# Last mixer of a two-block transformer on one core: the low parts of its weights formed by an accumulating DMA in SBUF

## The chip, the cores and the metric

The kernel runs on one NeuronCore of a Trainium2 chip. The metric is the device time of one launch in microseconds (us). The engines have these names in the profile: PE is TensorE, DVE is VectorE, ACT is ScalarE, POOL is GpSimd and SP is SyncE; PEld is the weight load of TensorE. A queue from which transfers are issued is called after its engine (SPq, POOLq).

## The reference, cut to what matters

Eight sublayers follow one another on 512 tokens of width 1024, all in fp32: MLA attention, feed-forward, differential attention, feed-forward, an even mixer, feed-forward, an odd mixer, feed-forward. The change concerns the odd mixer, the last of the four mixers:

```python
def odd_mixer(x, w_in, forget_b, dw_w, dw_b, cn_g, cn_b, w_out):
    p = x @ w_in
    q, k, v = ...                                     # 8 heads of 64 channels
    log_f = jax.nn.log_sigmoid(p[..., 3 * D_C:3 * D_C + H_C] + forget_b)
    y_c = forgetting_attention(q, k, v, log_f)        # logit += cum[t] - cum[s], causal
    y_d = conformer_conv(p[..., 3 * D_C + H_C:], dw_w, dw_b, cn_g, cn_b)
    return jnp.concatenate([y_c, y_d], axis=-1) @ w_out

def conformer_conv(p_d, dw_w, dw_b, cn_g, cn_b):
    h = p_d[..., :D_D] * jax.nn.sigmoid(p_d[..., D_D:])
    h = causal_dwconv(h, dw_w) + dw_b                 # 31 taps on each of 512 channels
    return jax.nn.silu(layer_norm(h, cn_g, cn_b))
```

## The kernel before, in words

Every fp32 product is made on TensorE from three products of a rounded high part and a remainder, the low part (lines 370 to 372: high times high, high times low, low times high). The weights come in units of 128 x 1024 (512 KB), or 128 x 528 (264 KB) for the first four units of the values. `Weights` keeps a plan of all units in the order of use. For each unit, `load` issues one transfer from DRAM into a raw tile on SP (line 162), and `split` makes the high part on ACT (line 169, a copy into the narrower type fp32r) and the low part (line 170, raw minus high) on DVE, for some units on POOL. The pool of raw tiles, `wraw`, has two buffers; `whi` and `wlo` have five each. So a raw tile is loaded when the one two units earlier has been read for the last time.

The odd mixer uses 26 such units after its first four. Those first four (`od_a` and `od_g` in the plan) and the next four named `od_x` are loaded from one tensor, `in_od_d`, for the convolution; then come `od_v` (values, four short units first and two long ones later), `od_q` and `od_k` (four head pairs each) and `od_o` (the output projection, eight). In the order of the plan: v 1 to 4 (short), x 1 to 4, q and k of pair 0, q and k of pair 1, v 5 and 6, q and k of pair 2, q and k of pair 3, o 1 to 8. In this text x 1 is the first `od_x` unit, q 0 the `od_q` unit of pair 0, and so on. All 26 low parts are made on DVE before.

Around them run these steps. `log_sigmoid` makes the log forget gates (an exponential on ACT, line 1480, then short DVE operations). `sums` adds them up with two matmuls (lines 1500 and 1501), ACT rounds the sums (`cumh`, line 1511), and `spread` writes them into the tiles `ab` on DVE (lines 1539 to 1542). `rows` transposes `ab` on PE (line 1549). `place` copies q and k of a head pair into stacked tiles: `qq` and `kb` by ACT (line 1418), the other half `kk` by a further ACT copy (line 1425). The scores of a head (lines 1588 to 1590) need all of these; ACT makes their softmax (lines 1603 and 1599) with short DVE operations between (lines 1602 and 1595), PE turns them over (line 1052) and multiplies them with the values.

The 124 taps of the convolution (lines 1368 and 1370, one DVE instruction each) lie between all this on DVE. A few run early; the rest stand behind `spread`. A scheduler that simulates the engines fixes the order of the instructions on each engine when the kernel is built; each engine then goes through its list strictly in that order, waiting on semaphores.

Of the kernel before, what the change touches and what calls it, by code (L numbers as in the profile page):

```python
# [9 lines left out]
F32 = mybir.dt.float32  # L10
F32R = mybir.dt.float32r
BF16 = mybir.dt.bfloat16
AF = mybir.ActivationFunctionType
OP = mybir.AluOpType
# [38 lines left out]

ONPOOL = ("uq_n", "ukv", "df_o", "mla_o")
OTHERWISE = (11, 12, 15, 20, 23, 24, 25, 73, 79, 80, 81, 82, 83, 84, 85, 86, 88, 90, 91, 100, 102, 103)
NORM_ACT = (1, 3, 6, 7, 12, 13, 16, 24, 25, 26, 30)
ROPE_POOL = (1, 2, 3, 4, 5, 7, 9, 11)
DUP_ACT = (0, 2, 4, 6)
# [83 lines left out]
class Weights:  # L142
# [23 lines left out]
    def split(self, pool, raw, o, n, eng):  # L166
        tiles = [p.tile([P, UNIT], F32R, name="w" + k, tag="w" + k) for p, k in zip(pool, ("hi", "lo"))]
        hi, lo = [x[:, :n] for x in tiles]
        self.nc.scalar.activation(hi, raw[:, o:o + n], AF.Copy)  # L169
        eng.tensor_sub(lo, raw[:, o:o + n], hi.bitcast(F32))  # L170
        return tiles

    def steps(self):

        while self.loaded < min(len(self.plan), self.at + 2) and (
                self.loaded == self.at or self.plan[self.loaded][0] != "win" or self.sums is not None):
            self.load()
        name, raw, n = self.got[self.at]
        self.at += 1
        nc = self.nc  # L180
        if name != "win":
            on_pool = (name in ONPOOL) != (self.at - 1 in OTHERWISE)
            self.ready.append((name, *self.split((self.hi, self.lo), raw[0], 0, n, nc.gpsimd if on_pool else nc.vector)))
            return

        gate, up = raw
        H = UNIT // 2
        a11, a12, a21, a22 = gate[:, :H], gate[:, H:], up[:, :H], up[:, H:]
        pg = self.split((self.hi, self.lo), gate, 0, UNIT, nc.vector)
        yield  # L190
        pu = self.split((self.hi, self.lo), up, H, H, nc.vector)
        nc.vector.tensor_add(a22, a21, a22)
        nc.vector.tensor_sub(a21, a11, a21)
        yield
        su = self.split(self.sums, up, 0, UNIT, nc.vector)
        nc.vector.tensor_sub(a11, a22, a11)
        nc.vector.tensor_sub(a12, a12, a11)
        yield
        sg = self.split(self.sums, gate, 0, UNIT, nc.vector)

        def part(tiles, o):
            return [x[:, o:o + H].rearrange("p (k n) -> p k n", n=P) for x in tiles]

        self.ready.append((name, {
            1: part(pg, 0), 2: part(pg, H), 3: part(sg, H), 4: part(pu, 0), 5: part(su, H), 6: part(sg, 0), 7: part(su, 0)}, None))
# [107 lines left out]
def kernel(ctx: ExitStack, tc: tile.TileContext, a: dict, out: bass.AP):  # L313
# [393 lines left out]
    def ffn(xpool_cm, xT, key, i, ps, names):  # L707
# [3 lines left out]
        with pool("ffn") as fp:  # L711
# [3 lines left out]
            def hidden(j, g, u):  # L715
                nc.vector.tensor_mul(g, g, u)
                h = fp.tile([P, S], F32R, name="hh", tag="hh", bufs=HID)
                l = fp.tile([P, S], F32R, name="hl", tag="hl", bufs=HID)
                split(h, l, g)
                chunks[j] = (h, l)  # L720
# [112 lines left out]
    def mla(xT, close_x, open_x, names):  # L833
        with pool("mla_o") as op_:
            cmask = op_.tile([P, S], F32, name="cmask")
            with ExitStack() as st:
# [28 lines left out]
                def turn_c(j, h, l):  # L865
                    ps = pst()
                    for t in range(NT):
                        nc.tensor.transpose(ps[:, t * P:(t + 1) * P], cq[:, t, j * P:(j + 1) * P], ident)
                    split(h, l, ps, par("g_q", j) if j < 3 else par("g_kv", j - 3))
# [67 lines left out]
                def head(h):  # L937
                    p, i = divmod(h, 2)
                    if i == 0:
                        WP[p] = W.next("uq_n", 3, 256), W.next("ukv", 2, 512)  # L940
                    wq, wk = WP[p]
                    m = slice(i * P, (i + 1) * P)
                    got = []
                    for s, (w, k, x, sc) in enumerate((
                            (wq, 3, (cqh, cql), -MLA_SCALE),
                            (wk, 2, (ckh, ckl), None))):
                        ps = acc()
                        project_T(ps, w, x, k, m=m)
                        hi = ap_.tile([P, S], F32R, name="qh", tag=f"qh{s}", bufs=2)
                        lo = ap_.tile([P, S], F32R, name="ql", tag=f"ql{s}", bufs=2)  # L950
                        split(hi, lo, ps, sc)
                        got += [hi, lo]
                    Q[h] = got
# [39 lines left out]
                def rest(h, pt, qb, n, e, sums):  # L993
                    nc.vector.reciprocal(sums[:, 2:3], sums[:, 1:2])
                    if 4 * h + qb in NORM_ACT:
                        nc.scalar.activation(e[:, :n], e[:, :n], AF.Copy, scale=sums[:, 2:3])
# [905 lines left out]
```

## Time and profile before

| | |
|---|---|
| median of 3 runs | 2256.09 us (2255.45 to 2257.32) |
| the profiled execution | 2255.44 us, of which the span from the first to the last instruction is 2253.7 us |
| mean granted clock of TensorE | 0.993 of full speed |
| PE busy | 2194.6 us, 97% of the span, 14076 matmuls |
| DVE busy | 1753.4 us, 78% |
| ACT busy | 998.2 us, 44% |
| POOL busy | 132.1 us, 6% |

The shares are means over the whole span. The profiled execution is 0.65 us below the median of the runs. The odd mixer occupies about 1660 to 1891 us of the span.

### The profile page before, as it was taken

To read this page: it belongs to the slowest core of one execution; us is meant where nothing else is said; L and a number is where in the kernel's file an instruction comes from. 1 tells how busy PE (TensorE), PEld (TensorE's weight loads), DVE (VectorE), ACT (ScalarE), POOL (GpSimd) and SP (SyncE) were. 2 spreads that over 40 slices of the span, in tenths; PEclk is the share of its full clock that TensorE was granted. 3 is DMA by queue.
4 is the path that set the end of the run, shared out by engine and by line. 5 is a ranking of instruction groups with operands and counts; after the bars stand their busy time and mean duration, and the time that the engine had idled before them with its cause. 6 is when DMAs were issued, how large, how long until landed. Compare 5 with 4: busy or idle time off the path is not lost. (4 is left out here: it accounts for less than half of the span.)

```text
span 2253.7 us, 35104 instructions
## 1 busy us (share of the span) xinstructions
PE 2194.6 (97%) x14076; PEld 1971.3 (87%) x14076; DVE 1753.4 (78%) x2871; ACT 998.2 (44%) x1669; POOL 132.1 (6%) x138
## 2 busy tenths in 40 slices
PE   8999999999999999999999999999999889999997
PEld 8888999998988789999988899999988767999996
DVE  5767988887666688888765588888679987988886
ACT  4654444333665554443333244433336655444331
POOL 2200000001321100000010000000010000000001
PEclk9999999999999999999999999999999899999999
DMA  5213332332321133333323233333232102233331
GB/s 174 64 48 103 94 113 94 113 94 75 111 79 63 47 108 107 104 94 113 94 98 95 75 131 107 104 100 108 90 99 93 57 19 103 94 113 94 113 94 56
DMA packets 59363, 210.48 MB, mean 93 GB/s; under 512 B 6624, under 2 KB 6880, under 8 KB 59200
## 3 DMA queue, kind: packets, MB, share of 16 engines
q1 hardware_dynamic: 56304, 198.97, 27.8%
q0 software_dynamic: 2320, 8.23, 1.1%
q8 instruction: 110, 1.80, 0.3%
q10 hardware_dynamic: 576, 1.05, 0.1%
q14 instruction: 53, 0.43, 0.1%
HBM read 206.12 MB, written 2.10 MB: 92 GB/s over the span
## 5 line engine op out<-in xcount | busy, mean ns | idle before, releaser
L169 ACT ACTIVATE whi<-wraw 128x1024 fp32r<-128x1024 f32 (+2 forms) x528 | 520.4, 988 | 838.8 <-PE acc L371 501.7
L170 DVE TENSOR_TENSOR wlo<-wraw,whi 128x1024 fp32r<-128x1024 f32 (+2 forms) x502 | 568.2, 1133 | 126.2 <-ACT whi L169 123.3
L371 PE MATMUL acc<-xl,whi 128*128 128x256 f32 (+1 forms) x1712 | 522.9, 305 | 3.5 <-DVE xl L480 3.5
L372 PE MATMUL acc<-xh,wlo 128*128 128x256 f32 (+1 forms) x1712 | 522.2, 305 | 2.6 <-DVE wlo L170 2.5
L370 PE MATMUL acc<-xh,whi 128*128 128x256 f32 (+1 forms) x1712 | 523.6, 306 | 0.4 <-DVE kl L1097 0.4
L371 PEld LDWEIGHTS acc<-xl,whi 128*128 128x128 f32 x1712 | 322.5, 188 | 29.2 <-DVE xl L480 4.7
L370 PEld LDWEIGHTS acc<-xh,whi 128*128 128x128 f32 x1712 | 322.4, 188 | 25.6 <-DVE kl L1097 0.5
L372 PE MATMUL acc<-xs,wlo 128*128 128x256 f32 x1216 | 341.3, 282 | 0.0
L371 PE MATMUL acc<-xql,whi 128*128 128x256 f32 x1216 | 341.0, 281 | 0.0
L372 PEld LDWEIGHTS acc<-xh,wlo 128*128 128x128 f32 x1712 | 322.6, 188 | 18.9 <-DVE wlo L170 3.8
L370 PE MATMUL acc<-xs,whi 128*128 128x256 f32 x1216 | 339.0, 280 | 0.0
L371 PEld LDWEIGHTS acc<-xql,whi 128*128 128x128 f32 x1216 | 228.5, 188 | 5.5
L370 PEld LDWEIGHTS acc<-xs,whi 128*128 128x128 f32 x1216 | 229.6, 189 | 3.5
L372 PEld LDWEIGHTS acc<-xs,wlo 128*128 128x128 f32 x1216 | 228.1, 188 | 0.3
L370 PE MATMUL tr<-whi,hh 128*128 128x512 f32 (+1 forms) x296 | 117.8, 398 | 0.0
L781 DVE TENSOR_TENSOR sums<-sums,acc 128x512 f32<-128x512 f32 x76 | 52.3, 688 | 83.9 <-PE acc L372 83.3
L371 PE MATMUL tr<-wlo,hh 128*128 128x512 f32 (+1 forms) x296 | 116.8, 395 | 0.0
L372 PE MATMUL tr<-whi,hl 128*128 128x512 f32 (+1 forms) x296 | 115.8, 391 | 0.0
L372 PE MATMUL ps<-whi,hl 128*128 128x512 f32 x288 | 113.7, 395 | 0.0
L370 PE MATMUL ps<-whi,hh 128*128 128x512 f32 x288 | 113.4, 394 | 0.0
L371 PE MATMUL ps<-wlo,hh 128*128 128x512 f32 x288 | 113.2, 393 | 0.0
L430 DVE SCALAR_TENSOR_TENSOR res<-res,acc 128x512 f32<-128x512 f32 x87 | 59.1, 683 | 58.1 <-PE acc L372 57.7
(364 smaller groups left out, 3959.5 us busy)
## 6 DMA issues: line engine op xcount, KB each, us to landing
wraw<-in_gu_dram SPq DMA_DIRECT2D x176, 512.0 KB, 3.5
wraw<-in_dn_dram SPq DMA_DIRECT2D x88, 512.0 KB, 3.4
wraw<-in_ev_in_dram SPq DMA_DIRECT2D x16, 512.0 KB, 3.5
wraw<-in_mla_o_dram SPq DMA_DIRECT2D x8, 512.0 KB, 3.5
wraw<-in_df_q_dram SPq DMA_DIRECT2D x8, 512.0 KB, 3.5
wraw<-in_df_k_dram SPq DMA_DIRECT2D x8, 512.0 KB, 3.5
wraw<-in_df_v_dram SPq DMA_DIRECT2D x8, 512.0 KB, 3.5
wraw<-in_df_o_dram SPq DMA_DIRECT2D x8, 512.0 KB, 3.4
```

The lines of the kernel that those rows point to most:

```text
L169: self.nc.scalar.activation(hi, raw[:, o:o + n], AF.Copy)
L170: eng.tensor_sub(lo, raw[:, o:o + n], hi.bitcast(F32))
L370: nc.tensor.matmul(ps, ah, bh, start=first, stop=False)
L371: nc.tensor.matmul(ps, ah, bl, start=False, stop=False)
L372: nc.tensor.matmul(ps, al, bh, start=False, stop=last)
L430: nc.vector.scalar_tensor_tensor(y, y, ALPHA if first else 1.0, ps, op0=OP.mult, op1=OP.add, accum_out=SUMS[t][:, c:c + 1] if sums else None)
L781: nc.vector.tensor_add(g[:, 1:3], g[:, 1:3], v)
```

## The change

For the five names of the odd mixer listed in `BYDMA`, the low part is no longer made by DVE. ACT writes minus the high part into the low tile (a copy with scale -1.0, from the raw tile), and a transfer issued on POOL's queue adds the raw tile to it, from SBUF to SBUF. Line numbers rise by 1 behind the new tuple and by 5 behind `split`.

```diff
+BYDMA = ("od_x", "od_v", "od_q", "od_k", "od_o")
...
         self.nc.scalar.activation(hi, raw[:, o:o + n], AF.Copy)
-        eng.tensor_sub(lo, raw[:, o:o + n], hi.bitcast(F32))
+        if eng is None:
+            self.nc.scalar.activation(lo, raw[:, o:o + n], AF.Copy, scale=-1.0)
+            self.nc.gpsimd.dma_start(lo.bitcast(F32), raw[:, o:o + n], accum_op=OP.add)
+        else:
+            eng.tensor_sub(lo, raw[:, o:o + n], hi.bitcast(F32))
...
-            self.ready.append((name, *self.split((self.hi, self.lo), raw[0], 0, n, nc.gpsimd if on_pool else nc.vector)))
+            self.ready.append((name, *self.split((self.hi, self.lo), raw[0], 0, n, None if name in BYDMA else nc.gpsimd if on_pool else nc.vector)))
```

The scheduler's order changes with it. On SP, these are the loads of v 3, v 4, x 1, x 2 and x 3 before (`DVE` in the waits is the low part of the unit two earlier, `DMAHW` an earlier load):

```order
L162 DMA wraw_16881<-in_od_v0_dram 128x528 [waits DMAHW7_49,DVE_49]
L162 DMA wraw_16887<-in_od_v0_dram 128x528 [waits DMAHW0_49,DVE_49]
L162 DMA wraw_17166<-in_od_d_dram 128x1024 [waits DMAHW1_49,DVE_49]
L162 DMA wraw_17196<-in_od_d_dram 128x1024 [waits DMAHW2_49,DVE_49]
L162 DMA wraw_17266<-in_od_d_dram 128x1024 [waits DMAHW3_49,DVE_49]
```

and the same loads in the changed kernel:

```order
L163 DMA wraw_16882<-in_od_v0_dram 128x528 [waits DMAHW7_49,DMASW1_49,Activation_49]
L163 DMA wraw_16889<-in_od_v0_dram 128x528 [waits DMAHW0_49,DMASW2_49,Activation_49]
L163 DMA wraw_17169<-in_od_d_dram 128x1024 [waits DMAHW1_49,DMASW3_49,Activation_49]
L163 DMA wraw_17200<-in_od_d_dram 128x1024 [waits DMAHW2_49,DMASW4_49,Activation_49]
L163 DMA wraw_17271<-in_od_d_dram 128x1024 [waits DMAHW3_49,DMASW5_49,Activation_49]
```

Their number and order stay; the semaphore of DVE is replaced by that of ACT and of the accumulating transfer (`DMASW`) that reads the raw tile.

On ACT, this is where the k parts of head pair 0 are placed, before (`whi_17700` is the high part of q 2, read from its raw tile `wraw_17640`):

```order
L169 ACTIVATE whi_17700<-wraw_17640 128x1024 [waits DMAHW5_49,PE_49]
L1418 ACTIVATE kb00_17069<-acc_17574 64x512 [waits PE_49]
L1418 ACTIVATE kb01_17073<-acc_17574 64x512
L1425 ACTIVATE kk00_17070<-kb00_17069 64x512 [waits Activation_49]
L1425 ACTIVATE kk01_17074<-kb01_17073 64x512 [waits Activation_49]
```

and in the changed kernel, where `whi_17655` and `wlo_17656` belong to v 6 and `whi_17714` and `wlo_17715` to q 2:

```order
L172 ACTIVATE wlo_17656<-wraw_17630 128x1024 [waits DMASW1_49]
L1423 ACTIVATE kb00_17072<-acc_17585 64x512 [waits PE_49]
L1423 ACTIVATE kb01_17076<-acc_17585 64x512
L170 ACTIVATE whi_17714<-wraw_17653 128x1024 [waits DMAHW5_49]
L172 ACTIVATE wlo_17715<-wraw_17653 128x1024 [waits DMASW2_49]
L1430 ACTIVATE kk00_17073<-kb00_17072 64x512 [waits Activation_49]
```

The high part of q 2 has moved from ahead of the `kb` copies to between them and the `kk` copies, and its negation stands there too.

On PE, this is where `rows` transposes `ab`, before (`whi_17433` is the high part of q 0):

```order
L370 MATMUL acc_17537<-xh_16571,whi_17433 128x512
L371 MATMUL acc_17537<-xl_16572,whi_17433 128x512
L1549 MATMUL tr_17442<-ident_76,ab1_17109 128x128 [waits DVE_49,Pool_49]
L1549 MATMUL tr_17437<-ident_76,ab0_17108 128x128 [waits DVE_49]
L1549 MATMUL tr_17437<-ident_76,ab0_17108 128x128 x3
```

and in the changed kernel (`whi_17322` is the high part of x 4):

```order
L375 MATMUL acc_17482<-xh_16571,whi_17322 128x512
L376 MATMUL acc_17482<-xl_16572,whi_17322 128x512
L1554 MATMUL tr_17451<-ident_76,ab1_17112 128x128 [waits DVE_49,Pool_49]
L1554 MATMUL tr_17446<-ident_76,ab0_17111 128x128 [waits DVE_49]
L1554 MATMUL tr_17446<-ident_76,ab0_17111 128x128 x3
```

The transposes have moved forward by more than a unit: from within the matmuls of q 0 to behind the first 8 of the 24 matmuls of x 4. In the same way the matmuls of `sums` have moved from x 3 to ahead of the last matmul of x 2, and on ACT `cumh` now stands behind the negation of k 0, the exponential of the gates behind that of x 3. On POOL the accumulating transfers of all units but the last stand, in the order of the plan, right behind the copy of `mkb` (line 1341 before, 1346 now).

## Rows read from the trace of the kernel before

**Rows 1.** The page: busy time of each engine.

```profile
PE 2194.6 (97%) x14076; PEld 1971.3 (87%) x14076; DVE 1753.4 (78%) x2871; ACT 998.2 (44%) x1669; POOL 132.1 (6%) x138
```

**Rows 2.** Stretches of the odd mixer: busy time of each engine, granted clock, DMA share.

```profile
core 0: us, PE busy (x) PEld busy (x) DVE busy (x) ACT busy (x) POOL busy (x), PEclk, DMA share, GB/s
...
1700.00:1778.50 78.50, 78.05 (x419) 65.02 (x417) 77.05 (x137) 51.09 (x98) 0.00 (x0) 1.00 0.26 81
1778.50:1781.90 3.40, 0.06 (x1) 0.00 (x0) 3.40 (x7) 3.35 (x7) 0.00 (x0) 0.94 0.00 0
1781.90:1795.10 13.20, 11.82 (x42) 9.63 (x42) 12.72 (x28) 8.93 (x22) 0.00 (x0) 0.50 0.15 41
1795.10:1844.20 49.10, 39.36 (x210) 29.20 (x208) 44.22 (x107) 32.02 (x92) 0.00 (x0) 0.96 0.00 1
1844.20:1870.00 25.80, 23.18 (x102) 18.62 (x103) 16.16 (x25) 9.21 (x12) 1.05 (x1) 0.93 0.26 82
```

**Rows 3.** Waits of PE, 1778 to 1845: total us, times, longest.

```profile
PE tr L1052 <- ACT e L1599: 5.1, 7, 1.3
PE ps L1588 <- ACT e L1603: 4.1, 5, 3.4
```

**Rows 4.** Waits of ACT in the same stretch.

```profile
ACT e L1599 <- DVE sums L1595: 8.6, 8, 1.9
```

**Rows 5.** Groups of DVE by line and shape, 1709 to 1845.

```profile
L1370 DVE SCALAR_TENSOR_TENSOR cv<-gl,sm,cv 128x512 f32<-128x512 f32 x98 | 69.4, 741 | 0.4
L170 DVE TENSOR_TENSOR wlo<-wraw,whi 128x1024 fp32r<-128x1024 f32 x12 | 14.6, 1215 | 0.0
```

**Rows 6.** Timeline of SP: start, duration, what is issued.

```profile
1672.41 11.17 SPq L162 DMA_DIRECT2D wraw<-in_od_d_dram  x4
1685.71 10.82 SPq L162 DMA_DIRECT2D wraw<-in_od_qk_dram  x4
```

**Rows 7.** Timeline of DVE; the idle time before in brackets.

```profile
1671.67 0.71 DVE L170 TENSOR_TENSOR wlo<-wraw,whi 128x528 fp32r<-128x528 f32 x1 [2.13 <-ACT whi L169]
...
1684.46 1.22 DVE L170 TENSOR_TENSOR wlo<-wraw,whi 128x1024 fp32r<-128x1024 f32 x1
...
1708.94 0.27 DVE L1542 TENSOR_TENSOR ab<-cumh,lf 128x64 f32<-128x64 f32 x1
```

**Rows 8.** Timeline of ACT.

```profile
1668.15 0.65 ACT L169 ACTIVATE whi<-wraw 128x528 fp32r<-128x528 f32 x1 [5.44 <-PE acc L371]
...
1679.99 1.06 ACT L169 ACTIVATE whi<-wraw 128x1024 fp32r<-128x1024 f32 x1 [1.63 <-DMA wraw<-in_od_d_dram]
...
1708.27 0.23 ACT L1511 ACTIVATE cumh<-lf 128x32 fp32r<-128x32 f32 x1 [1.23 <-DVE lf L1510]
...
1726.39 1.27 ACT L1425 ACTIVATE kk<-kb 64x512 fp32r<-64x512 f32 x2
```

**Rows 9.** Timeline of POOL.

```profile
1663.62 0.82 POOL L1341 CAST mkb<-cst 128x128 bf16<-128x128 f32 x1 [2.59 <-DMA cst<-in_cst_dram]
```

**Rows 10.** Transfers: count, KB each, median us from issue to landing; and SP's loads as a share.

```profile
q1 hardware_dynamic: 56304, 198.97, 27.8%
...
wraw<-in_od_d_dram SPq DMA_DIRECT2D x8, 512.0 KB, 3.5
...
lng<-in_ln_ffn_g_dram POOLq DMA_DIRECT2D x4, 512.0 KB, 4.8
...
wraw<-in_od_v_dram SPq DMA_DIRECT2D x4, 264.0 KB, 2.7
```

**Rows 11.** Timeline of PE: matmuls 7, 8 and 9 of x 4; the first use of `kk`.

```profile
1706.88 0.40 PE L370 MATMUL acc<-xh,whi 128*128 128x512 f32 x1
1707.12 0.40 PE L371 MATMUL acc<-xl,whi 128*128 128x512 f32 x1
1707.35 0.40 PE L372 MATMUL acc<-xh,wlo 128*128 128x512 f32 x1
...
1729.15 0.22 PE L1589 MATMUL ps<-kk,qq 128*128 128x128 f32 x1
```

**Rows 12.** Timeline of PE: the first score behind its longest wait.

```profile
1781.94 0.47 PE L1588 MATMUL ps<-kb,qa 128*128 128x128 f32 x1 [3.38 <-ACT e L1603]
```

## The prediction, made before the changed kernel ran

> **What bounds the kernel now.** I began with the busy times of the page: PE is busy 97% of the span and DVE 78% [rows 1]. These are means over eight sublayers, so the next view cuts the odd mixer into stretches [rows 2]. From 1700 to 1778.5 us two engines are full at once: PE works 78.05 of 78.5 us and DVE 77.05. PE sets the pace there; DVE is full because the convolution's taps, which nobody needs yet, fill every gap. Up to 1778.5 DVE is therefore no bound, and whatever is taken from it there buys no time at that place.
>
> Behind it PE loses time. In the three stretches from 1778.5 to 1844.2 it stands still for 3.3 + 1.4 + 9.7 = 14.5 us, and the granted clock costs more: 13.2 us at 0.50, the lower of its two levels (1.2 against 2.4 GHz), lose 6.6 us and 49.1 us at 0.96 lose 2.0. Together that is 23.1 us [rows 2]. The half-clock stretch follows a single wait of PE of 3.38 us [rows 12]. PE's waits there are named: for the normed exponentials of ACT 5.1 us, for ACT's exponential itself 4.1 us [rows 3]. ACT in turn waits 8.6 us, in 8 waits, for the reciprocal on DVE [rows 4], a tiny operation that stands in DVE's list between taps: 98 taps (69.4 us) and 12 low parts (14.6 us) run on DVE from 1709 to 1845 [rows 5]. Here, and only here, a relieved DVE can shorten the kernel.
>
> The third view is the timelines around the loads. The low part of v 3 ends at 1671.67 + 0.71 = 1672.38, that of x 3 at 1685.68 [rows 7], and SP issues the next load into the same raw tile 0.03 us later in both cases (1672.41 and 1685.71) [rows 6]. So SP waits for nothing but the last reader of a raw tile, and of those there are two. One turn of a raw tile now takes a load (3.5 us [rows 10]), a high part (1.06 [rows 8]) and a low part (1.22 [rows 5]), 5.8 us; two tiles give a unit every 2.9 us at best, and PE takes one every 24 x 0.23 = 5.6 us (matmuls follow 0.23 us apart [rows 11]). The prologue has twice what it needs.
>
> **The change part by part.** DVE loses 26 low parts, 22 of 1.22 us and 4 of 0.71. Up to 1778.5 this is worth nothing, as said. ACT gains 26 negations; I cost one like the high part, the same copy of the same tile: 1.06 us, 0.65 for a short unit [rows 8]. ACT is busy 51.09 of 78.5 us [rows 2], so that its time as such hides; its order is what counts (below). POOL only issues; it is busy 6% [rows 1] and its transfers stand in the order of the units.
>
> The real edit is to the turn of a raw tile. It is now: load 3.5, high 1.06, negation 1.06, and then the landing of the accumulating transfer, which I call L (L' for a short unit): L + 5.62. No row shows such a transfer. The bounds: not below the 3.5 us that SP's 512 KB take; not above twice the 4.8 us of a plain 512 KB on POOL's queue, 9.6 [rows 10]. Between them I start from 4.8, the same queue, size and issuing engine, and add a second reading of the bytes, since the operation must read the low tile as well as the raw tile. SP's 198.97 MB took 27.8% of the 16 engines' span of 2253.7 us, so 0.524 MB cost 0.278 x 2253.7 x 0.524 / 198.97 = 1.65 us [rows 10]. L = 6.45; with half of that addition L' = 5.65. A unit then comes every (6.45 + 5.62) / 2 = 6.0 us, against the 5.6 that PE takes: the prologue no longer overtakes PE.
>
> The Trainium skill states in "Collectives: The Full Stack", "Why ReduceScatter is half of AllGather", that an adding transfer is slower because it reads two sources (measured 62.28 against 32.35 GB/s). No row here shows an adding transfer; an estimate that puts this whole ratio on 4.8 us gives 9.3 us, and the sum would be about 2291.
>
> A slower prologue costs time where something on PE's path stands behind it. Low parts do not: by the second chain below that of q 1 is there at 1690.9 + 2L' + 4L = 1728, where PE is due at some 1722.5 (65 matmuls of 0.23 us behind the one at 1707.35 [rows 11]) and late itself by then. But ACT works in order, and two of its copies now stand behind negations:
>
> First, `cumh` stands behind the negation of k 0. That unit's raw tile goes v 2, v 4, x 2, x 4, k 0. The high part of v 2 is made at 1668.15, held by PE [rows 8], so its negation ends at 1669.45; four turns later, 2L' + 2L + 4.0 + 3 x 5.62 (a short load of 2.7 [rows 10], 0.65 and 0.65 in the first), k 0 is negated at 1690.3 + 2L' + 2L. Then `cumh`, 0.23, and `spread`, from 1708.27 to 1709.21 in all 0.94 [rows 7, 8]: 1691.5 + 2L' + 2L = 1715.7. PE wants the transposes of `ab` behind the eighth matmul of x 4, at 1707.4 [rows 11]: a wait of 8.3 us. (The matmuls of `sums`, earlier in PE's list, wait for the gates, behind the negation of x 3; that wait is a part of the 8.3 and not additional.)
>
> Second, `kk` of pair 0 stands behind the negation of q 2. Its raw tile goes v 1, v 3, x 1, x 3, q 0, q 1, v 5, q 2. POOL's first transfer can't be issued before the copy of `mkb` ends at 1664.44 [rows 9]. Seven turns: 1664.44 + 4.0 + 6 x 5.62 + 2L' + 5L = 1702.2 + 2L' + 5L, then 0.64 for the copy (half of two in 1.27 [rows 8]): 1746.35. PE needs it at 1729.15 [rows 11]: 17.2 us in all, of which 8.3 are waited for already. Behind q 2 the heads use a unit more slowly than 6 us, so that the loop falls behind no further.
>
> PE so takes two waits of over 8 us. Long waits lowered the clock here: the one of 3.38 us was followed by 6.6 us of loss, and the stretch from 1844.2, at 0.93 of 25.8 us, lost 1.8 [rows 2, 12]. I take the middle, 4.2, twice: 8.4 us.
>
> On the other side, from 1709 to 1845 DVE is rid of 14.6 us [rows 5], so the taps end earlier and the reciprocals come sooner. Of the 23.1 us lost there the whole can come back at most; part of the waits are ACT's own exponentials, which nothing shortens [rows 3]. I take half, 11.6 us.
>
> Sum against the profiled execution: 2255.4 + 17.2 + 8.4 - 11.6 = 2269.4. That execution is 0.65 us below the median, so the median is predicted at 2270.
>
> **The rivals.** *A quick transfer (the other side).* If adding costs nothing beyond the plain 4.8, the two waits shrink to 3.3 and 7.25 us in all. They cost the clock little (1.8 each), and since PE is barely late, DVE's relief arrives nearly whole in the heads, say 20 us: 2255.4 + 7.25 + 3.6 - 20 = 2246. For it: SP's transfers, at 3.5, are even faster, and 16 engines are used by a quarter there [rows 2, 10]. The point from which it decides: with 11.6 returned and 3.6 lost by the clock, the wait must stay below 8.0 us, which is L of about 5.1. The Trainium skill ("DMA: Bandwidth & Descriptors", "Anatomy of one DMA — SWDGE (gpsimd) path") fits 2.0 us + bytes / 436e3, an estimate of 3.2 us for 512 KB; by it this rival holds, but the trace's 4.8 on this queue is above it.
>
> *A slow transfer.* L = L' = 9.6: 1702.8 + 2 x 9.6 + 5 x 9.6 = 1770.0, a wait of 40.9 us; 2255.4 + 40.9 + 8.4 - 11.6 = 2293. For it: no row shows what adding costs in the transfer engines; against it: they stand idle for three quarters of that time.
>
> *The tail gives back everything.* The waits are as I say, but the heads lose nothing any more, since DVE had been the last of their causes: 2255.4 + 17.2 + 8.4 - 23.1 = 2258, no change. For it: ACT's 8.6 us behind DVE [rows 4] and the single 3.38 us wait whose clock loss is the largest piece. Against it: ACT gives PE its waits by name [rows 3], and it gets more work.
>
> **How the numbers follow.** My forecast has a chance of 0.46, the quick transfer 0.20, the slow one 0.17, the full return 0.17. Within 0.2% (4.5 us, about what a measurement of this kernel can tell from no change) falls most of the full return, and some of the quick one and of mine: 0.17. Faster: most of the quick transfer and a little of the full return, 0.22. Slower 0.61. The range goes from 2247 to 2292, which leaves out about half of the quick case and half of the slow one. The forecast's own range, by half or double the clock loss and a quarter to three quarters of the return, is 2260 to 2280.
>
> **What would show it.** The landing of the accumulating transfers decides: 6.45 us supports the sum, 5 or less the quick rival, 9 or more the slow one. SP should issue each load right behind such a landing, and ACT's high parts should wait for loads where they waited for PE. PE should show a wait of some 8 us at the matmuls of `sums` and the transposes of `ab` together, another of 9 at `kk` of pair 0, and half clock behind them. In the heads PE's idle time should be near 7 us instead of 14.5, with fewer waits of ACT for reciprocals. I am wrong if PE keeps its 99% up to the first scores, or if low parts, and not copies on ACT, are what it waits for.

## The result and the profile after

The changed kernel takes 2273.02 us (median of 4 runs, 2272.26 to 2273.76) against 2256.04 us before: a ratio of 1.0074, 95% interval [1.0057, 1.0092]. It is slower by 17 us, as forecast (2270). The profiled execution took 2272.56 us with a span of 2270.8 us.

The page's first line, as [rows 1]: DVE has lost 26 us of work, ACT gained 21 and POOL 22, and PE does the same work in a longer time.

```profile
PE 2196.6 (97%) x14076; PEld 1973.0 (87%) x14076; DVE 1727.2 (76%) x2845; ACT 1019.6 (45%) x1695; POOL 154.0 (7%) x164
```

The stretches of the odd mixer, with the columns of [rows 2], are cut anew, since PE's work comes later. By PE's timeline, v 5 is first used at 1765 us here and was at 1736 before; the stretches up to 1765 hold what is ahead of it:

```profile
1660.00:1700.00 40.00, 37.98 (x281) 35.80 (x280) 17.62 (x33) 17.63 (x26) 8.83 (x19) 1.00 0.62 148
1700.00:1718.40 18.40, 11.38 (x49) 8.37 (x47) 10.16 (x36) 8.02 (x9) 2.13 (x3) 0.99 0.73 164
1718.40:1740.00 21.60, 21.57 (x91) 17.78 (x92) 16.84 (x27) 12.49 (x17) 2.34 (x3) 0.93 0.75 171
1740.00:1765.00 25.00, 13.74 (x50) 9.87 (x50) 18.49 (x32) 17.47 (x28) 3.44 (x4) 0.74 0.63 147
1765.00:1800.00 35.00, 35.00 (x219) 30.64 (x219) 30.49 (x61) 28.96 (x60) 4.30 (x5) 0.99 0.56 138
1800.00:1861.50 61.50, 53.29 (x281) 42.12 (x280) 51.48 (x127) 48.71 (x127) 2.58 (x3) 0.92 0.24 58
```

In the four stretches up to 1765 PE is idle for 2.0 + 7.0 + 0.0 + 11.3 = 20.3 us, and the granted clock (0.99, 0.93 and 0.74 in the last three) costs another 0.2 + 1.5 + 6.5 = 8.2. Before, nearly nothing was lost there (0.4 us idle from 1660 to 1736, at full clock). In the heads (1800 to 1861.5) 8.2 us are idle and 4.9 lost by the clock, 13.1 together, against the 23.1 of before: 10 us have come back.

PE's waits from 1660 to 1765 (total, times, longest):

```profile
PE tr L1554 <- DVE ab L1545: 5.6, 1, 5.6
PE ps L1594 <- ACT kk L1430: 4.8, 1, 4.8
PE ps L1593 <- ACT kb L1423: 4.0, 1, 4.0
PE ps L1593 <- ACT e L1608: 2.5, 1, 2.5
PE acc L377 <- DMA wlo<-wraw: 2.3, 2, 1.6
PE ps L1505 <- PE acc L376: 0.8, 1, 0.8
```

The first wait is for `ab`, behind `cumh`; the next two are for the placing of k of pair 0, and the 2.5 us behind them for the first exponentials of the heads. The low parts themselves cost 2.3 us. The cause stands one view further, in the timelines of SP, POOL and ACT:

```profile
1704.31 20.83 SPq L163 DMA_DIRECT2D wraw<-in_od_qk_dram  x4
...
1704.14 0.86 POOL L173 DMA_DIRECT2D wlo<-wraw  x1 [5.71 <-ACT wlo L172]
1711.14 0.86 POOL L173 DMA_DIRECT2D wlo<-wraw  x1 [6.13 <-ACT wlo L172]
1717.99 1.04 POOL L173 DMA_DIRECT2D wlo<-wraw  x1 [5.99 <-ACT cumh L1516]
...
1715.69 1.06 ACT L170 ACTIVATE whi<-wraw 128x1024 fp32r<-128x1024 f32 x1 [4.85 <-DMA wraw<-in_od_qk_dram]
1716.65 1.04 ACT L172 ACTIVATE wlo<-wraw 128x1024 fp32r<-128x1024 f32 x1
1717.60 0.21 ACT L1516 ACTIVATE cumh<-lf 128x32 fp32r<-128x32 f32 x1
...
1748.72 1.06 ACT L170 ACTIVATE whi<-wraw 128x1024 fp32r<-128x1024 f32 x1 [3.29 <-DMA wraw<-in_od_qk_dram]
1749.68 1.04 ACT L172 ACTIVATE wlo<-wraw 128x1024 fp32r<-128x1024 f32 x1
1750.74 1.28 ACT L1430 ACTIVATE kk<-kb 64x512 fp32r<-64x512 f32 x2
```

The four loads of q and k take 20.83 us where they took 10.82 [rows 6]. ACT waits for the load of k 0, makes its high part and negation, and only then `cumh`; the same with q 2 and `kk`. Before, the high part of k 0 waited for PE and not for a load:

```profile
1693.86 1.06 ACT L169 ACTIVATE whi<-wraw 128x1024 fp32r<-128x1024 f32 x1 [1.20 <-PE acc L371]
```

POOL's rows show a second thing: each accumulating transfer is issued at the same moment as a load, since the landing that frees one raw tile and the negation of the other fall together. SP's four loads, merged in its row, are issued at 1704.31, 1711.24, 1718.14 and 1724.81, each within 0.2 us of a transfer. The view of the low tiles gives the landings of the transfers issued from 1700 to 1730, and of those from 1855 to 1877, where few loads run:

```profile
DMA to landing us min/median/max: 6.8/7.0/8.3
...
DMA to landing us min/median/max: 4.4/4.5/6.3
```

### The profile page after: what moved, and what is told of

Read it like the earlier page. It is cut to its first block, busy times and chain, and to the rows that moved or that the text cites. A ratio compares the mean times of both kernels' runs of the same rounds, so it can differ in the third digit from the quotient of the medians.

```text
span 2270.8 us, 35167 instructions
## 1 busy us (share of the span) xinstructions
PE 2196.6 (97%) x14076; PEld 1973.0 (87%) x14076; DVE 1727.2 (76%) x2845; ACT 1019.6 (45%) x1695; POOL 154.0 (7%) x164
## 3 DMA queue, kind: packets, MB, share of 16 engines
q0 software_dynamic: 6064, 20.84, 4.0%
## 5 line engine op out<-in xcount | busy, mean ns | idle before, releaser
L175 DVE TENSOR_TENSOR wlo<-wraw,whi 128x1024 fp32r<-128x1024 f32 (+2 forms) x476 | 538.6, 1132 | 115.0 <-ACT whi L170 114.2
L393 POOL TENSOR_TENSOR lnr<-lnv,mhalf 128x1 f32<-128x1 f32 x32 | 24.4, 761 | 1274.2 <-DVE lnv L391 1274.1
```

The costliest lines, as they stand in the source:

```text
L393: nc.gpsimd.tensor_tensor(r[:, :n], v[:, :n], mhalf[:, :n], op=OP.pow)
```

## The experiments

The theory: with an accumulating transfer a raw tile is held until the transfer has landed; there are two; so the loads come every 6.8 us, and two copies on ACT that PE needs stand behind negations that wait for loads ("tile held"). The rivals: the 26 negations on ACT and the scheduler's new order do it ("negations"), or the adding as such is so slow that the transfer engines are the limit ("price of adding"). The expectations use this last name in two senses: the transfer is long because it adds, or the engines' own time is what the kernel waits for. Only the second contradicts the theory.

**Without the transfers.** In `split`, low parts stay minus the high part:

```diff
             self.nc.scalar.activation(lo, raw[:, o:o + n], AF.Copy, scale=-1.0)
-            self.nc.gpsimd.dma_start(lo.bitcast(F32), raw[:, o:o + n], accum_op=OP.add)
```

> The changed kernel without the accumulating transfers: the low parts of these 26 units stay minus the high part, so the low products are left wrong and only the time is read. Theory 'tile held': the raw tile is free after the negation, a turn is 5.6 us for two tiles, PE's waits at the sums, the transposes and kk vanish (under 2 us together) and DVE's relief stays: about 2246 us (2236 to 2251). Rival 'negations': the waits stay, 2265 or more.

Measured: 2246.84 us, 0.9958 of before [0.9943, 0.9973]. PE's waits from 1660 to 1765 are these two:

```profile
PE acc L376 <- DVE wlo L174: 0.4, 1, 0.4
PE ps L1592 <- ACT e L1607: 0.3, 1, 0.3
```

All 26 negations are there. The scheduler's order differs from the changed kernel's, but `cumh` and `kk` stand behind negations here too (of q 1 and q 2). So the negations make none of the waits, the relief of DVE, less whatever the negations cost, is worth 9 us, and the transfers cost 26.

**A plain copy in place of the adding one.**

```diff
-            self.nc.gpsimd.dma_start(lo.bitcast(F32), raw[:, o:o + n], accum_op=OP.add)
+            self.nc.gpsimd.dma_start(lo.bitcast(F32), raw[:, o:o + n])
```

> The changed kernel with a plain copy from SBUF to SBUF in place of the adding one, on the same queue and of the same size: the low parts become copies of the raw tile, so only the time is read. Theory 'tile held, queueing behind the load': packets fall from 328 ns to some 165, which takes 128 x 163 / 16 = 1.3 us from a landing of 7.0 us; the first packet still comes 3.2 us after the issue; seven turns shorten by 9 us and the time falls to about 2262 (2257 to 2267). Rival 'price of adding': the landing falls to 4.2 us or less also while a load runs, the front waits vanish: about 2247.

Measured: 2252.88 us, 0.9986 [0.9977, 0.9996]; the landings from 1700 to 1730, and what is left of PE's front waits:

```profile
DMA to landing us min/median/max: 2.8/3.7/3.9
...
PE ps L1594 <- ACT kk L1430: 2.6, 1, 2.6
PE tr L1554 <- DVE ab L1545: 1.6, 1, 1.6
```

The order of the instructions on PE, ACT and DVE is that of the changed kernel, so the new order alone does not make the 17 us: with a landing of 3.7 instead of 7.0 us the same order runs 20 us faster. My expectation of 2262 missed, because I had taken the queueing behind a load as fixed. It is not: with the shorter turn a copy is issued 0.9 us or more behind a load (1708.42 against 1707.52) and no longer with it.

The landing fell as the rival 'price of adding' had it, in its first sense (the time did not fall to its 2247): the transfer is long in part because it adds. POOL's queue (packets, MB, share of the 16 engines' span) before, in the changed kernel and with the plain copy:

```profile
q0 software_dynamic: 2320, 8.23, 1.1%
...
q0 software_dynamic: 6064, 20.84, 4.0%
...
q0 software_dynamic: 5808, 20.84, 2.6%
```

For the same 12.6 MB more, adding takes 2.9 points of the engines' time and copying 1.5.

**Half of each transfer.**

```diff
-            self.nc.gpsimd.dma_start(lo.bitcast(F32), raw[:, o:o + n], accum_op=OP.add)
+            self.nc.gpsimd.dma_start(lo.bitcast(F32)[:, :n // 2], raw[:, o:o + n // 2], accum_op=OP.add)
```

> The changed kernel with accumulating transfers of half the columns; the other half of each low part stays minus the high part, so only the time is read. It asks how the landing of 7.0 us is made up. If mostly by queueing behind the load that is issued at the same moment, the first packet still comes 3.2 us after the issue and the landing is still 5.3 us or more: front waits shorten by some 12 us, 2258 to 2263. If mostly by the adding of the bytes themselves, the landing falls to 4 us or less and with it nearly all front waits: 2248 to 2254.

Measured: 2255.39 us, 0.9994 [0.9984, 1.0004]. The landings from 1700 to 1730:

```profile
DMA to landing us min/median/max: 3.5/4.1/5.6
```

Half of the bytes take 2.9 us off the landing, more than half of the 4.5 that a transfer takes where few loads run. Both forecasts missed, the time lies between them: this run changes the bytes and the meeting with a load at once, for here too the transfers are issued 0.7 us or more behind a load (1704.25 against 1703.49). The packets in the changed kernel's trace part the two. Of the transfer issued at 1704.14 none moves for 3.5 us; from 1704.2 to 1707.6 the load's queue is the only one with packets:

```profile
q1 hardware_dynamic: 102, 0.42, 59.9%
```

The first packet comes 3.2 to 3.5 us after the issue for the four transfers issued with a load from 1697 to 1718, and 1.4 for that of 1858, which meets none. So some 2 of the 2.5 us between 4.5 and 7.0 are queueing behind the load, and the landing of 7.0 is not a price per byte alone.

**The same sums, with the raw tile free.** The transfer adds the weights from DRAM again instead of from the raw tile, which then has its last reader in the negation. The DRAM tensor is read as fp32r.

```diff
-            self.nc.gpsimd.dma_start(lo.bitcast(F32), raw[:, o:o + n], accum_op=OP.add)
+            self.nc.gpsimd.dma_start(lo, self.plan[self.at - 1][1][0].bitcast(F32R), accum_op=OP.add)
```

> The changed kernel with the same 26 accumulating transfers, but their source is the weights in DRAM instead of the raw tile, so that the raw tile is free behind the negation. Theory 'tile held': a turn no longer contains a landing; the front waits of 20 us fall under 5 and the time to about 2248 us (2243 to 2255), although the transfer engines move more. Rival 'price of adding' in the sense that the engines' time itself is the limit: the waits stay, 2265 or more. Rival 'negations': 2268 to 2274.

Measured: 2249.56 us, 0.9972 [0.9962, 0.9981]. The landings from 1700 to 1730 are no shorter, and yet PE's front waits are small:

```profile
DMA to landing us min/median/max: 6.2/7.2/8.1
...
PE ps L1594 <- ACT qq L1423: 1.8, 1, 1.8
PE tr L1554 <- DVE ab L1545: 1.4, 1, 1.4
```

This run decides between holding and price: the same number of accumulating transfers, as slow as in the changed kernel and with 4.3% of the engines' span for the same 20.84 MB on POOL's queue, cost little once no raw tile waits for them: 2.7 us more than no transfers at all. The order is planned anew here as well, but `cumh` and `kk` again stand behind the negations of q 1 and q 2, no earlier than in the changed kernel.

**Three raw tiles.** For the room, one low tile less; the control is the kernel before with the same counts.

```diff
-    wraw = ctx.enter_context(tc.tile_pool(name="wraw", bufs=2))
+    wraw = ctx.enter_context(tc.tile_pool(name="wraw", bufs=3))
...
-    wlo = ctx.enter_context(tc.tile_pool(name="wlo", bufs=5))
+    wlo = ctx.enter_context(tc.tile_pool(name="wlo", bufs=4))
```

> The changed kernel with three raw tiles instead of two (and four low tiles instead of five, for the room). Theory 'tile held': the accumulating transfer (7.0 us from issue to landing in the prologue) holds one of only two raw tiles, and the copies on ACT stand behind negations that wait for the next load. With three tiles a unit can come every (7.0 + 5.6) / 3 = 4.2 us against the 5.6 that PE takes, so that the waits of PE at the sums, the transposes of ab and kk fall from 20 us to under 4, and what DVE gives back in the heads stays: about 2247 us (2240 to 2255). Rival 'negations': the 26 negations on ACT and the new order make the waits, whatever the transfer takes: 2268 to 2274. Rival 'price of adding' (the transfer is slow because it adds, not because it queues behind the loads): the same as the first here.

> The kernel before with the same two buffer counts (three raw tiles, four low tiles), as the control. All theories: the prologue of before has twice the pace it needs, so 2256 us within 4.

Measured: 2259.89 us, 1.0018 [1.0009, 1.0027], against 2254.14 us for the control, 0.9991 [0.9982, 1.0000]. Better than two tiles by 13 us, but a miss by all theories. PE's largest front wait, and ACT and SP before it:

```profile
PE ps L1593 <- ACT kb L1423: 6.3, 1, 6.3
...
1712.78 1.06 ACT L170 ACTIVATE whi<-wraw 128x1024 fp32r<-128x1024 f32 x1
...
1726.56 1.06 ACT L172 ACTIVATE wlo<-wraw 128x1024 fp32r<-128x1024 f32 x1
...
1732.39 0.33 SPq L163 DMA_DIRECT2D wraw<-in_od_qk_dram  x1
1738.53 1.06 ACT L170 ACTIVATE whi<-wraw 128x1024 fp32r<-128x1024 f32 x1 [5.99 <-DMA wraw<-in_od_qk_dram]
```

The tile of k 1 is read for the high part at 1712.78, but its negation stands 14 us further down ACT's list, and only behind that transfer can q 2 be loaded (1732.39), whose high part stands ahead of the `kb` copies. Again a held raw tile, this time held by the negation. Whether four low tiles made the scheduler place it so late was not separated; three raw tiles with five low ones were not run. The run also bears out the queueing: its four transfers issued from 1700 to 1730, each 1.6 us or more from the nearest issue of a load, are of full size and land in 4.8 at the median, not 7.0:

```profile
DMA to landing us min/median/max: 4.4/4.8/5.0
```

**Which units.** Three runs change one line each: `BYDMA = ("od_o",)`, `BYDMA = ("od_x", "od_v")`, and, in the kernel before, `"od_o"` added to `ONPOOL`.

> Only the eight units of the output projection by accumulating transfer; the 18 units ahead of them as before. Theory 'tile held': the prologue keeps its pace, PE has no wait at the sums, the transposes of ab or kk; DVE is rid of 5 low parts between 1750 and 1785 us, ahead of the stretch where PE waits for the heads, so some of the 23 us lost there come back: about 2251 us (2246 to 2256). Rival 'negations': ACT, which PE waits for in the heads, gets 5 more instructions there and 3 behind: 2256 to 2262.

> Only the ten units named od_x and od_v by accumulating transfer; q, k and the output projection as before. Theory 'tile held': the first eight units are paced by the transfers, so x 3 and x 4 come late and with them the gates, the sums and the transposes (3 to 6 us of PE's waits there), but kk of pair 0 hangs on no negation of q 2; DVE's relief lies mostly ahead of 1700 us, where it is worth nothing: 2260 us (2255 to 2265). Rival 'negations': 10 negations, all ahead of the heads, where ACT has room: 2256 within 3.

> The kernel before with the eight low parts of the output projection on POOL's vector unit in place of DVE: no transfer, no work for ACT. If the gain of a relieved DVE in the heads is real, about 2251 us (2246 to 2256), as in the run with the late units by transfer; if the heads are bound by ACT alone, 2256 within 3.

Measured: the late units alone 2253.00 us, 0.9988 [0.9979, 0.9998]; the early ones alone 2263.54 us, 1.0034 [1.0021, 1.0047]; the late ones on POOL 2255.87 us, 1.0000 [0.9991, 1.0009]. PE's waits with the early units by transfer, from 1660 to 1765, then the low parts on POOL and ACT's waits in that run, 1760 to 1845:

```profile
PE tr L1554 <- DVE ab L1545: 3.3, 1, 3.3
PE acc L377 <- DMA wlo<-wraw: 2.3, 2, 2.0
PE ps L1594 <- DVE kk L1426: 2.0, 1, 2.0
```

```profile
L170 POOL TENSOR_TENSOR wlo<-wraw,whi 128x1024 fp32r<-128x1024 f32 x8 | 22.2, 2777 | 175.0 <-PE tr L1052 87.7 <-ACT whi L169 81.1 <-PE ps L1589 3.8
...
ACT e L1599 <- DVE sums L1595: 9.7, 7, 3.1
ACT e L1603 <- DVE sums L1602: 9.1, 6, 3.9
```

The early units alone lose 7 of the 17 us; q and k were not run alone with the raw tile as the source, so where the rest falls is not separated. The late ones lose nothing and bring 3 us; both lie in the ranges expected. The run on POOL has the time that would speak for ACT as the bound, but it does not test that, for DVE was not relieved in it: five low parts fewer (6.1 us) run on DVE from 1709 to 1845, and its 98 taps take 7.1 us more than in [rows 5]:

```profile
L1370 DVE SCALAR_TENSOR_TENSOR cv<-gl,sm,cv 128x512 f32<-128x512 f32 x98 | 76.5, 815 | 0.3
```

The ten taps that ran while POOL made a low part took 1.47 us on average, the other 88 took 0.74.

**The version that beats both.** From DRAM, as above, but for q, k and the projection only, the early units on DVE: `BYDMA = ("od_q", "od_k", "od_o")`.

> Accumulating transfers with DRAM as their source for q, k and the output projection only (16 units); x and v on DVE as before. If what helps is DVE's relief shortly ahead of the heads, and what hurts is the held raw tile, this keeps the first and drops the second and the early negations that brought nothing: 2247 us (2242 to 2252), no slower than the variant with all 26 units from DRAM. If the early relief of DVE counted too, 2250 to 2256.

Measured: 2247.91 us, 0.9961 [0.9946, 0.9976], as good as the run without any transfer. Beside the variant with all 26 units from DRAM (0.9972) the intervals overlap; that leaving out the early units helps by itself is not shown. Beside the late units alone (2253.00) it is 5 us faster, with q and k added and the source changed; which of the two does it is not separated.

## Why the prediction was right, point by point

**What bounds the kernel.** Right as far as the runs go. The time that DVE spends on the low parts of x and v is worth nothing that shows: the last run leaves it to DVE and is no slower than the one with all 26 units from DRAM. In the heads a relief is worth something: PE is idle there for 8.2 us where it was for 14.5, and 9 us are gained without transfers. ACT's waits for reciprocals there were 8.6 us [rows 4], and 0.6 for the row minima. ACT's waits for DVE in the changed kernel, from 1765 to 1862:

```profile
ACT e L1608 <- DVE sums L1607: 4.7, 4, 1.8
...
ACT e L1604 <- DVE sums L1600: 0.9, 1, 0.9
```

The reciprocals (line 1600 now) are nearly in time; a part of the wait has moved to the row minima (line 1607), the operation ahead of the exponential, and that I had not foreseen. In all, the 9.2 us are 5.6 now.

**The turn of a raw tile.** Right in kind: SP issues each load behind a landing, 6.8 us apart, against the 6.0 of the sum. L was mis-sized only a little, 6.45 against 7.0, but by the wrong terms. I had made it of a plain 4.8 us and 1.65 for a second reading. A transfer that runs nearly alone takes 4.5 us in all; most of the rest is queueing behind the load of the other tile, which is issued at the same moment. The load is slower beside it too, 4.2 where I had 3.5, a term that I had left as it was before. For the short units I had 5.65; they landed in 3.4 at the median:

```profile
wraw<-in_od_qk_dram SPq DMA_DIRECT2D x8, 512.0 KB, 4.2
...
wlo<-wraw POOLq DMA_DIRECT2D x22, 512.0 KB, 5.1
wlo<-wraw POOLq DMA_DIRECT2D x4, 264.0 KB, 3.4
```

The errors of L and L' go against each other: 2 x 5.65 + 5 x 6.45 = 43.6 in the sum, 2 x 3.4 + 5 x 7.0 = 41.8 by the measured rows. That the sum of waits came out is in part luck. The statement of the Trainium skill ("Collectives: The Full Stack", "Why ReduceScatter is half of AllGather") points the right way: for the same bytes adding took the transfer engines 2.9 points of their time and the plain copy 1.5, a ratio of 1.9; whether a second reading makes it, no run shows. The landings, 7.0 against 3.7, are no such measure, since only the adding transfers were issued together with loads. The use of the ratio on 4.8 us, which gave 9.3, is refuted. The fit in "DMA: Bandwidth & Descriptors", "Anatomy of one DMA — SWDGE (gpsimd) path" (an estimate of 3.2 us) is near the plain copy's 3.7 and not near an adding transfer's 7.0.

**The two waits.** Predicted 8.3 us for `sums` and `ab` together and 17.2 in all up to `kk`. Measured: 0.8 + 5.6 for the two, 2.3 for low parts, 4.0 + 4.8 at the placing of k: 17.5. One step was wrong: low parts were waited for, 2.3 us. One was incomplete: the `kb` copies, and not only `kk`, came late. The first score that uses `kk` ran at 1729.15 [rows 11] and runs here at

```profile
1751.42 0.47 PE L1594 MATMUL ps<-kk,qq 128*128 128x128 f32 x1 [4.84 <-ACT kk L1430]
```

The 2.5 us for the first exponentials behind it stand in no term of the sum.

**The clock.** 8.4 us predicted, as 4.2 twice; 8.2 measured, as 1.7 around the first wait and 6.5 around those for `kb` and `kk`. That the two add up to the forecast is luck. The measured figure counts the lowered clock over idle time too and is somewhat too high.

**What comes back.** 11.6 us predicted, 10 by idle time and clock; PE's idle time in the heads is 8.2 us where I had expected some 7. Sum of the parts measured: 20.3 + 8.2 - 10 = 18.5, against 17.1 by which the span grew; before, too, half a microsecond was idle in the front. The positions of the same PE instruction in the two traces give a second account: the changed kernel is 1.5 us late before the odd mixer begins, where the two do not differ, 27.5 us late where the trace of before stands at 1745, and 17.3 at 1891. So some 26 us are lost ahead of the heads and 10 come back.

The slow and the quick transfer are excluded by the landings, the full return by the heads. One figure of the quick rival does not come out: by its own terms, with 1702.8 + 7 L against 1729.15, a wait of 8.0 us belongs to an L of about 4.9, not 5.1. No term of the sum uses it.

## What to carry to other kernels

Before a transfer takes over the work of an engine, look at which buffer it reads and who waits to refill it: an operation of 1.2 us became one of 7, and with two buffers that is the pace of the whole chain. An engine's list is in order, so a short operation that has to wait for such a buffer stops all that stands behind it, even if its own time is nothing. Taking the second operand from where nobody waits for the buffer (here from DRAM again) turned 17 us of loss into 7 us of gain with the same number of transfers.

## What the runs showed of the hardware

A transfer from SBUF to SBUF of 512 KB that adds landed 4.5 us after its issue where few loads ran, and 7.0 where one of SP's loads of 512 KB was issued within 0.2 us of it; the first packet came 1.4 and 3.2 to 3.5 us after the issue. The plain copy, issued 0.9 us or more behind a load, landed in 3.7. Adding took the transfer engines about twice the time of copying. POOL's issue takes 0.86 us for an adding transfer and 0.54 for the plain copy. POOL's subtraction of a 128 x 1024 tile takes 2.78 us against 1.22 on DVE [rows 5], and the taps on DVE that ran beside it took 1.47 us on average instead of 0.74.
